# Boundary chains of four token blocks emitted one step behind each other, with last groups of four k-tiles and two-block splits

## The chip, the cores and the metric

One core of one Trainium2 chip runs the whole program. The metric is the time of one execution in device microseconds (us). Engines are named as in the profile: PE (TensorE matmul), PEld (its weight loads), DVE (VectorE), ACT (ScalarE), POOL (GpSimd), SP (SyncE, which issues most DMA). The profile lists PE's granted clock as a share of full speed: 1.00 and 0.50 are 2.4 and 1.2 GHz.

## The reference, cut to what matters

512 tokens of 1024 values go through two blocks of two layers each. That makes eight stages in a row, each ending in a projection back to 1024 values:

```
x = x + rmsnorm(ssd(rmsnorm(x)))        # ssd    first block: the stage's output is normalised
x = x + rmsnorm(conv_ffn(rmsnorm(x)))   # ffn0   before it is added
x = x + rmsnorm(rglru(rmsnorm(x)))      # lru
x = x + rmsnorm(conv_ffn(rmsnorm(x)))   # ffn1
h = h + even(rmsnorm(h))                # even   second block: plain residual
h = h + conv_ffn_2(rmsnorm(h))          # ffn2
h = h + mla(rmsnorm(h))                 # mla
h = h + conv_ffn_2(rmsnorm(h))          # ffn3
out = rmsnorm(h)
```

So between any two stages every token needs the sum of its squares over all 1024 values before the next stage's first matmul can use it. At the ends of ssd, ffn0, lru and ffn1 it needs that twice in a row: once over the stage's output, once over the new x. These four are called the double boundaries below, the ends of even, ffn2 and mla the single ones.

## The kernel before, in words

**Matmuls.** Each fp32 operand is split into a high and a low fp32r part, and a product is three passes: high by high, low by high, high by low (`mm3`, L413 to L417, weights stationary, tokens moving; `mmt`, L534 to L536, tokens stationary, used for the down projections `dn`).

**Weights.** The class `Weights` (`W`) streams chunks of 1 MB in a fixed order on SP's queue. `_half` casts half of a chunk to its high part `wh` (L283 on ACT, or L285 on DVE) and subtracts for the low part `wl` (L286 on DVE or POOL). `W.main` says on which engines, by a list of two-letter plans: the first letter is the engine of `wh`, the second that of `wl` (a is ACT, v is DVE, g is POOL). The default is `av`; lru has `vg`. The parts live in a pool of seven buffers (`wsp`), so they are made only shortly before use.

**Down projections.** A stage's projection back is summed over k-tiles of 128 rows in groups (`G_SSD`, `G_LRU`, `G_FF` and so on). All groups but the last are added into `acc` (or into `x` in the second block) over all tokens. The last group has two k-tiles at most boundaries and is done by `last_down` one block q of 128 tokens at a time, two halves of 512 columns each.

**The boundary.** `stage_end` does, for each token block q: the last group's matmuls `dn(q)`; the add into `acc` on DVE (L411); the sum of squares on ACT (`sq`, L494, one instruction for each half); the inverse root on POOL (`rr`, L496 and L497); `nx` on DVE (L592) and the add to x (L411); squares of x, `rr` again; the normalised block `n` on ACT (L513); eight 128x128 transposes on PE (L516); and the split of each transposed tile into `xh` on ACT (L521) and `xl` on DVE (L522), 128x128 each. At single boundaries the chain is shorter: `dn` is added to x, then squares, `rr`, `n`, transposes, splits. The next stage's first three weight tiles (`units`) are then multiplied in two halves of 256 tokens: half 0 needs blocks 0 and 1, half 1 needs blocks 2 and 3.

Emission order in the code before is:

```
dn(0) dn(1) newx(0) dn(2) newx(1) dn(3) newx(2)
units, half 0        newx(3)        units, half 1
```

where `newx(q)` is the whole chain of block q from its squares of `acc` to its splits. A scheduler may move instructions past one another where tiles allow it, but on each engine the four blocks' chains stand largely one after another.

**Other places.** At the start, x is loaded on SP between the first weight halves, and the same transposes, splits and units follow. At the end, `final_end` does the last projection and the output norm block by block.

Of the kernel before, what the change touches and what calls it, by code (L numbers as in the profile page):

```python
# [16 lines left out]
P = 128  # L17
# [230 lines left out]
class Weights:  # L248


    def __init__(self, c, ap):
        self.c, self.ap, self.n = c, ap, ap.shape[0]
        self.used, self.count, self.halves, self.raw = [], {}, [], None
        self.look, self.done = 2, 0
        self.main = self.plan = ("av",)
        self.until = 0

# [13 lines left out]
    def _half(self):  # L271
# [5 lines left out]
        hi = c.wsp.tile([P, T], F32R, name="wh", tag="wh")  # L277
        lo = c.wsp.tile([P, T], F32R, name="wl", tag="wl")
# [11 lines left out]
    def ahead(self, n):  # L290
        while self.done < min(n, 2 * self.n):
            self._half()

# [38 lines left out]
def build(tc, nc, aps, at, stages):  # L332
# [4 lines left out]
    with ExitStack() as st:  # L337
# [25 lines left out]
        for q in range(4):  # L363
            for h in range(2):
                nc.sync.dma_start(x[q][:, h * T:h * T + T], aps["x"][q][:, h * T:h * T + T])
            W.load_half(q)
# [123 lines left out]
        def rms_rows(src):  # L490

            ss = small.tile([P, 2], F32, name="ss", tag="ss")
            for h in range(2):
                A.activation(tmp("sq"), src[h], AF.Square, scale=1.0 / 32, accum_out=ss[:, h:h + 1])  # L494
# [5 lines left out]
        class Entry:  # L500
# [7 lines left out]
            def put(self, q):  # L508
                rr = rms_rows([half(x, q, h) for h in range(2)])
                qs = slice(q * P, q * P + P)  # L510
                for h in range(2):
                    n = tmp("n")
                    A.activation(n, half(x, q, h), AF.Identity, scale=rr)  # L513
                    ps = mmps(c.tp)
                    for e in range(4):
                        PE.transpose(ps[:, e * P:e * P + P], n[:, e * P:e * P + P], ident)  # L516
                    for e in range(4):
                        hi, lo = self.xs[4 * h + e]
                        gk = vc(self.gain, 4 * h + e)
                        pe = ps[:, e * P:e * P + P]  # L520
                        A.activation(hi[:, qs], pe, AF.Identity, scale=gk)  # L521
                        V.scalar_tensor_tensor(lo[:, qs], pe, gk, hi[:, qs].bitcast(F32),  # L522
                                               op0=ALU.mult, op1=ALU.subtract)

        def units_half(uc, up, xs, h):
            for u, ps in zip(uc, up):
                for k in range(KD):
                    mm3(ps[:, HALF[h]], u.blk(k), cut(xs[k], HALF[h]), k == 0, k == KD - 1)
# [37 lines left out]
        def last_down(name, hs, acc):  # L566

            n = len(hs)
            W.look = 0
            c.dn = "dn" if "dn" in c.psb else "ax"  # L570
            ws = parts_of(name, 2 * n)

            def dn(q):
                for h in range(2):
                    ps = mmps(c.dn)
                    for k in range(n):
                        mmt(ps, hs[k], q, ws[n * h + k], k == 0, k == n - 1)
                    tt(half(acc, q, h), ps, half(acc, q, h), ALU.add)
            return dn

        def stage_end(name, hs, acc, g, nxt, units, xo=None):
# [3 lines left out]
            dn = last_down(name, hs, acc)  # L585

            def newx(q):
                if g is not None:
                    rr = rms_rows([half(acc, q, h) for h in range(2)])
                    for h in range(2):  # L590
                        t = tmp("nx")
                        V.scalar_tensor_tensor(t, half(acc, q, h), rr, g[h],  # L592
                                               op0=ALU.mult, op1=ALU.mult)
                        tt(half(x, q, h), t, xo[2 * q + h] if xo else half(x, q, h), ALU.add)
                nxt.put(q)
# [12 lines left out]
            W.look = 2  # L608
            return up

        def final_end(name, hs):
# [4 lines left out]
            def outs(q):  # L616
                rr = rms_rows([half(x, q, h) for h in range(2)])
                for h in range(2):
                    o = tmp("o")
                    V.scalar_tensor_tensor(o, half(x, q, h), rr, g[h],  # L620
                                           op0=ALU.mult, op1=ALU.mult)
                    nc.sync.dma_start(aps["out"][q][:, h * T:h * T + T], o)
            for q in range(4):
                dn(q)
                outs(q)
# [44 lines left out]
        def ssd(pl, ent, pre, fin):  # L670
# [101 lines left out]
            def core(g, qd, bc, xc, zs, gated):  # L772
# [97 lines left out]
                if g < 3:  # L870
                    def dn():
                        for n, d in enumerate(down("sout", hs, acc, copy_first if g == 0 else None)):

# [3 lines left out]
                else:  # L877
                    drain(down("sout", hs[:2], acc))
                    st_.hs = hs[2:]
# [46 lines left out]
            for k in range(8):  # L926
                t = pl.tile([P, T], F32, name="xo", tag="zs" if k < 7 else "xc", bufs=7 if k < 7 else 5)
# [5 lines left out]
        def lru(pl, ent, pre, fin):  # L933
# [67 lines left out]
            def dense():  # L1001
# [11 lines left out]
                for q, grp in enumerate((range(4), range(4, 8), range(8, 10))):  # L1013
# [3 lines left out]
                    for h in grp:  # L1017
# [5 lines left out]
                        hs.append(split(pl, t, "hs", bufs=7))  # L1023
# [800 lines left out]
```

## Time and profile before

| what | value |
|---|---|
| time, median of 3 runs | 2987.62 us (2987.57 to 2993.34) |
| profiled execution, time | 2990.36 us |
| its span | 2988.6 us |
| mean granted PE clock | 0.979 |
| PE busy | 2870.8 us, 96% |
| DVE busy | 1878.0 us, 63% |
| ACT busy | 1291.0 us, 43% |
| POOL busy | 416.6 us, 14% |

The profiled execution is 2.74 us above the median of the runs; its own time and its span differ by 1.8 us, which lie around the program. PE is busy nearly all the time, so time can come out of the program only where PE waits, where its clock is granted at the lower level, or where it does less work.

### The profile page before, as it was taken

The page shows a single profiled execution, that of the slowest core. Times are in us where ns is not written, and L with a number is a line of the kernel's source. Part 1 is how long each engine was busy: PE and PEld are TensorE (multiplying, and loading weights), DVE is VectorE, ACT ScalarE, POOL GpSimd, SP SyncE. Part 2 cuts the span into 40 slices and gives each one's busy share as a digit, 9 for nine tenths or more (in the row PEclk, how much of TensorE's full clock was granted, in tenths as well). Part 3 has the DMA queues.
Part 4 walks back from the last instruction along what each step waited for, and adds up shares of the span by engine and source line. Part 5 has one row for each costly group of instructions (what it writes and reads, how often), then busy time and mean ns, then how long its engine had stood idle before and what let it go on. Part 6 is the DMA issues. An engine that isn't in the chain of part 4 may idle for free.

```text
span 2988.6 us, 35753 instructions
## 1 busy us (share of the span) xinstructions
PE 2870.8 (96%) x13528; PEld 2347.7 (79%) x13528; DVE 1878.0 (63%) x3120; ACT 1291.0 (43%) x2366; POOL 416.6 (14%) x524
## 2 busy tenths in 40 slices
PE   8999997999999799799999998999999999999998
PEld 7767777888888677688878877888888876788887
DVE  6887776555655786586665764666545566655544
ACT  5444445433333562444333444655333364453332
POOL 1233210000000146302342311100000000000000
PEclk8999998999999899899999998999999999999999
DMA  3212231222222122123333334622222220132222
GB/s 135 71 57 71 71 106 71 99 98 89 96 99 99 64 85 99 61 103 109 111 135 121 124 114 146 196 82 85 99 99 99 85 89 29 57 105 93 99 88 89
DMA packets 100188, 285.74 MB, mean 96 GB/s; under 512 B 19632, under 2 KB 28336, under 8 KB 99504
## 3 DMA queue, kind: packets, MB, share of 16 engines
q1 hardware_dynamic: 89376, 272.15, 26.0%
q10 hardware_dynamic: 10640, 11.30, 1.2%
q8 instruction: 107, 1.75, 0.2%
q14 instruction: 65, 0.53, 0.1%
HBM read 269.31 MB, written 14.12 MB: 95 GB/s over the span
## 4 chain that ended last, share of the span: by engine, by line
PE 86%; DVE 7%; ACT 4%; POOL 2%; issue 1%; DMA 1%; SPq 0%; DVEq 0%; POOLq 0%; ACTq 0%
PE mm L415 18%; PE mm L416 17%; PE mm L417 17%; PE dn L535 6%; PE dn L534 6%; PE dn L536 6%; PE mm L534 2%; PE mm L535 2%; PE mm L536 2%; ACT sq L494 1%; ACT n L513 1%; DVE wl L286 1%; POOL rr L497 1%; PE ax L1656 1%; PE ax L1678 1%
## 5 line engine op out<-in xcount | busy, mean ns | idle before, releaser
L283 ACT CAST wh<-raw 128x512 fp32r<-128x512 f32 x870 | 537.5, 622 | 1114.8 <-PE mm L416 711.5
L415 PE MATMUL mm<-xh,wh 128*128 128x512 f32 (+1 forms) x2600 | 982.7, 381 | 5.5 <-DVE co L633 3.4
L417 PE MATMUL mm<-xh,wl 128*128 128x512 f32 (+1 forms) x2600 | 980.5, 378 | 7.5 <-POOL wl L286 7.5
L416 PE MATMUL mm<-xl,wh 128*128 128x512 f32 (+1 forms) x2600 | 980.1, 378 | 2.7 <-DVE xl L522 2.7
L286 DVE TENSOR_TENSOR wl<-raw,wh 128x512 fp32r<-128x512 f32 x870 | 633.8, 735 | 501.2 <-ACT wh L283 485.4
L415 PEld LDWEIGHTS mm<-xh,wh 128*128 128x128 f32 x2600 | 496.3, 192 | 99.7 <-issue 7.3
L417 PEld LDWEIGHTS mm<-xh,wl 128*128 128x128 f32 x2600 | 496.9, 191 | 96.9 <-POOL wl L286 8.8
L416 PEld LDWEIGHTS mm<-xl,wh 128*128 128x128 f32 x2600 | 496.8, 191 | 90.7 <-DVE xl L522 3.8
L534 PE MATMUL dn<-wh,hsh 128*128 128x512 f32 x864 | 339.3, 393 | 2.6 <-DVE acc L411 2.6
L535 PE MATMUL dn<-wl,hsh 128*128 128x512 f32 x864 | 340.7, 394 | 0.3 <-DVE wl L286 0.3
L536 PE MATMUL dn<-wh,hsl 128*128 128x512 f32 x864 | 335.8, 389 | 0.0
L496 POOL TENSOR_SCALAR rr<-ss 128x1 f32<-128x1 f32 x52 | 16.3, 314 | 1554.8 <-ACT sq L494 1554.7
L534 PEld LDWEIGHTS dn<-wh,hsh 128*128 128x128 f32 x864 | 162.2, 188 | 41.0 <-DVE acc L411 3.0
L536 PEld LDWEIGHTS dn<-wh,hsl 128*128 128x128 f32 x864 | 162.2, 188 | 35.9
L535 PEld LDWEIGHTS dn<-wl,hsh 128*128 128x128 f32 x864 | 162.5, 188 | 32.9 <-DVE wl L286 0.7
L633 DVE SCALAR_TENSOR_TENSOR ca<-mm,vec,ca 128x510 f32<-128x510 f32 x216 | 161.6, 748 | 16.1 <-ACT ca L630 12.5
L411 DVE TENSOR_TENSOR acc<-dn,acc 128x512 f32<-128x512 f32 x128 | 87.6, 686 | 83.7 <-PE dn L536 83.4
L411 DVE TENSOR_TENSOR x<-dn,x 128x512 f32<-128x512 f32 x96 | 66.0, 689 | 101.6 <-PE dn L536 101.6
L286 POOL TENSOR_TENSOR wl<-raw,wh 128x512 fp32r<-128x512 f32 x66 | 104.2, 1597 | 92.5 <-DVE wh L285 73.0
L633 DVE SCALAR_TENSOR_TENSOR cb<-mm,vec,cb 128x510 f32<-128x510 f32 (+1 forms) x128 | 95.7, 748 | 9.8 <-ACT cb L630 7.9
L429 ACT CAST hsh<-act 128x512 fp32r<-128x512 f32 x108 | 67.2, 622 | 77.9 <-DVE act L411 77.8
L630 ACT ACTIVATE ca<-mm,vec 128x512 f32<-128x512 f32 x108 | 83.8, 776 | 11.3 <-PE mm L417 11.3
(482 smaller groups left out, 3284.9 us busy)
## 6 DMA issues: line engine op xcount, KB each, us to landing
raw<-w SPq DMA_DIRECT2D x233, 1024.0 KB, 4.8
sD<-s5t SPq DMA_DIRECT2D x4, 1024.0 KB, 7.4
row<-rows SPq DMA_DIRECT2D x12, 256.0 KB, 5.2
sR<-s5t SPq DMA_DIRECT2D x4, 768.0 KB, 4.3
x<-x SPq DMA_DIRECT2D x8, 256.0 KB, 5.5
xo<-x ACTq DMA_DIRECT2D x8, 256.0 KB, 3.4
s5t<-el ACTq DMA_DIRECT2D x8, 256.0 KB, 3.2
s5t<-HD ACTq DMA_DIRECT2D x4, 512.0 KB, 3.1
```

Source lines behind the costliest of these rows:

```text
L283: c.nc.scalar.copy(hi, r)
L286: (c.nc.gpsimd if e[1] == "g" else c.nc.vector).tensor_tensor(lo, r, hi.bitcast(F32), op=ALU.subtract)
L411: (eng or V).tensor_tensor(o, a, b, op=op)
L415: PE.matmul(ps, lhsT=wh, rhs=xh, start=first, stop=False)
L416: PE.matmul(ps, lhsT=wh, rhs=xl, start=False, stop=False)
L417: PE.matmul(ps, lhsT=wl, rhs=xh, start=False, stop=last)
L429: A.copy(hi, src)
L534: PE.matmul(ps, lhsT=hh[:, qs], rhs=wh, start=first, stop=False)
L535: PE.matmul(ps, lhsT=hh[:, qs], rhs=wl, start=False, stop=False)
L536: PE.matmul(ps, lhsT=hl[:, qs], rhs=wh, start=False, stop=last)
L630: A.activation(o, src, AF.Identity, scale=w[nt - 1], bias=b)
L633: V.scalar_tensor_tensor(o[:, d:], src[:, :T - d], w[j], o[:, d:], op0=ALU.mult, op1=ALU.add)
```

## The change

The work is the same: the same matmuls, the same norms, the same splits. What differs is where it stands:

- **Last groups.** `G_SSD` goes from (4, 4, 4, 2, 2) to (4, 4, 4, 4), `G_LRU` from (4, 4, 2) to (4, 2, 4), ffn0 and ffn1 end in a group of four k-tiles in place of two groups of two. The other lists are as they were, so at the single boundaries the last group still has two.
- **Homes for weights.** A last group of four needs eight weight halves at once, more than the pool's seven buffers. `reserve` and `last_homes` give them tiles of the stage that are free by then, and `W.more()` makes the parts ahead, one or two with each step of the group before.
- **stage_end** is taken apart into `a` (matmuls, add, squares of one half), `b` (nx, x, squares), `n`, `t` (transposes) and `parts` (splits), and these are emitted so that each block stands one step behind the block before it.
- **Transposes** of two token blocks go into the same four PSUM tiles, two k-tiles to a tile, and `parts(h)` splits 128x256 at a time: 8 on ACT and 8 on DVE for each half of the tokens, where there were 16 and 16 of 128x128.
- **units**: at double boundaries the transposes of block 2 stand between the second and third unit of half 0; at single ones after the first unit.
- **Start and end**: x is loaded two blocks ahead of each pair of weight halves, and the pieces are emitted like a boundary; in `final_end` the output of a block stands after the next block's first half.
- **lru's plan** goes from `vg` to `av` and `vv` in turn: `wl` always on DVE, `wh` half on ACT, half on DVE.

```diff
-G_SSD = _groups(4, 4, 4, 2, 2)
-G_LRU = _groups(4, 4, 2)
+G_SSD = _groups(4, 4, 4, 4)
+G_LRU = _groups(4, 2, 4)
-G_FF = {FF1: _groups(*(4,) * 7, 2, 2), FF2: _groups(*(4,) * 5, 2)}
+G_FF = {FF1: _groups(*(4,) * 8), FF2: _groups(*(4,) * 5, 2)}
...
+    def reserve(self, n, tiles):
+
+        for k, t in enumerate(tiles):
+            self.homes[2 * n + k] = t
...
-        hi = c.wsp.tile([P, T], F32R, name="wh", tag="wh")
-        lo = c.wsp.tile([P, T], F32R, name="wl", tag="wl")
+        if h in self.homes:
+            hi, lo = self.homes.pop(h)()
+        else:
+            hi = c.wsp.tile([P, T], F32R, name="wh", tag="wh")
+            lo = c.wsp.tile([P, T], F32R, name="wl", tag="wl")
...
+    def more(self, n=1):
+        self.ahead(self.done + n)
...
+            def turn(self, q, n):
+
+                if q % 2 == 0:
+                    self.tp = [mmps(t) for t in c.tp[q // 2]]
                 for k in range(KD):
+                    o = (k % 2) * 256 + (q % 2) * P
+                    PE.transpose(self.tp[k // 2][:, o:o + P], n[k // 4][:, (k % 4) * P:(k % 4) * P + P], ident)
+
+            def parts(self, h):
+                for k in range(KD):
+                    hi, lo = self.xs[k]
+                    gk = vc(self.gain, k)
+                    pe = self.tp[k // 2][:, (k % 2) * 256:(k % 2) * 256 + 256]
+                    A.activation(hi[:, HALF[h]], pe, AF.Identity, scale=gk)
+                    V.scalar_tensor_tensor(lo[:, HALF[h]], pe, gk, hi[:, HALF[h]].bitcast(F32),
+                                           op0=ALU.mult, op1=ALU.subtract)
...
-            dn(0)
-            dn(1)
-            newx(0)
-            dn(2)
-            newx(1)
-            dn(3)
-            newx(2)
-            uc = [W.next(u) for u in units]
-            up = [mmps() for _ in units]
-            units_half(uc, up, nxt.xs, 0)
-            newx(3)
-            units_half(uc, up, nxt.xs, 1)
-            W.look = 2
-            return up
...
+            if g is not None:
+                a(0, 0), a(0, 1), a(1, 0), b(0), a(1, 1), n(0), a(2, 0), b(1), a(2, 1), t(0), n(1)
+                a(3, 0), t(1), b(2), a(3, 1), nxt.parts(0), n(2), b(3)
+
+                def rest():
+                    n(3), t(3), nxt.parts(1)
+                return first_units(nxt, units, [lambda: None, lambda: t(2)], rest)
+            a(0, 0), a(0, 1), a(1, 0), n(0), a(1, 1), a(2, 0), t(0), n(1), a(2, 1), a(3, 0), t(1)
+            n(2), nxt.parts(0), a(3, 1), n(3)
+
+            def rest():
+                t(3), nxt.parts(1)
+            return first_units(nxt, units, [lambda: t(2)], rest)
...
-        PLAN = {"lru": ("vg",)}
+        PLAN = {"lru": ("av", "vv")}
```

**ACT at the boundary from ffn0 to lru.** In the kernel before, these rows stand together; x1 and acc2 are token blocks 1 and 2, `n_8144` and `n_8159` are the two halves of block 1's normalised x:

```order
L494 ACTIVATE sq_8137,ss_8136<-x1_83 128x512
L494 ACTIVATE sq_8139,ss_8136<-x1_83 128x512
L513 ACTIVATE n_8144<-x1_83,rr_8141 128x512
L513 ACTIVATE n_8159<-x1_83,rr_8141 128x512
L494 ACTIVATE sq_8191,ss_8190<-acc2_4325 128x512
L494 ACTIVATE sq_8193,ss_8190<-acc2_4325 128x512
L521 ACTIVATE xh0_4301<-ax_8146,vec_81 128x128
L521 ACTIVATE xh4_4309<-ax_8161,vec_81 128x128
```

The squares of block 2's `acc` stand behind block 1's `n`. In the changed kernel ACT has, at the same place:

```order
L531 ACTIVATE n_7972<-x0_82,rr_7946 128x512
L531 ACTIVATE n_7974<-x0_82,rr_7946 128x512
L506 ACTIVATE sq_7991,ss_7976<-acc2_4261 128x512
L506 ACTIVATE sq_8001,ss_7997<-x1_83 128x512
L506 ACTIVATE sq_8006,ss_7997<-x1_83 128x512
L506 ACTIVATE sq_8025,ss_7976<-acc2_4261 128x512
L531 ACTIVATE n_8046<-x1_83,rr_8008 128x512
L531 ACTIVATE n_8048<-x1_83,rr_8008 128x512
```

Block 2's squares now stand ahead of block 1's `n`. A little later on ACT, the splits of half 0 and block 2's `n` stand so:

```order
L548 ACTIVATE xh3_4243<-mm_8035,vec_81 128x256
L506 ACTIVATE sq_8084,ss_8075<-x2_84 128x512
L506 ACTIVATE sq_8103,ss_8050<-acc3_4262 128x512
L531 ACTIVATE n_8124<-x2_84,rr_8086 128x512
L531 ACTIVATE n_8126<-x2_84,rr_8086 128x512
L548 ACTIVATE xh5_4247<-mm_8036,vec_81 128x256
L548 ACTIVATE xh7_4251<-ax_8037,vec_81 128x256
```

Two of the eight splits that half 0 needs, xh5 and xh7, come behind block 2's `n`.

**PE at the boundary from ffn0 to lru.** Before, the last down matmuls and the transposes of blocks 0 and 1 stand directly ahead of the first unit:

```order
L536 MATMUL dn<-wh,hsl 128x512
L516 MATMUL ax<-ident,n 128x128 x4
L534 MATMUL dn<-wh,hsh 128x512
L516 MATMUL ax<-ident,n 128x128 x4
L535 MATMUL dn<-wl,hsh 128x512
L536 MATMUL dn<-wh,hsl 128x512
L516 MATMUL ax<-ident,n 128x128 x8
L415 MATMUL mm<-xh_4301,wh 128x256 x3
```

All down matmuls are used up by the time that block 1's eight transposes come. In the changed kernel the end of the down projection reads:

```order
L560 MATMUL dn<-w_7836,hsh 128x512
L561 MATMUL dn<-w_7836,hsh 128x512
L562 MATMUL dn<-w_7836,hsl 128x512
L541 MATMUL mm<-ident,n 128x128 x6
L541 MATMUL ax<-ident,n 128x128 x2
L560 MATMUL dn<-w_7853,hsh 128x512
L561 MATMUL dn<-w_7853,hsh 128x512
L562 MATMUL dn<-w_7853,hsl 128x512
L560 MATMUL dn<-w_7862,hsh 128x512
L561 MATMUL dn<-w_7862,hsh 128x512
L562 MATMUL dn<-w_7862,hsl 128x512
```

Block 1's transposes are shown here; three more down matmuls follow these rows, then the first unit. Block 0's transposes stand 15 down matmuls further ahead, with 72 down matmuls (all of blocks 0, 1 and 2) ahead of them.

**PE at the single boundary from ffn2 to mla.** Before, between block 1's transposes and the first unit:

```order
L535 MATMUL dn<-wl,hsh 128x512
L516 MATMUL ax<-ident,n 128x128 x8
L536 MATMUL dn<-wh,hsl 128x512
L534 MATMUL dn<-wh,hsh 128x512
L535 MATMUL dn<-wl,hsh 128x512
L536 MATMUL dn<-wh,hsl 128x512
L415 MATMUL mm<-xh_17112,wh 128x256 x2
L416 MATMUL mm<-xl_17113,wh 128x256
```

In the changed kernel:

```order
L541 MATMUL mm<-ident,n 128x128 x6
L541 MATMUL ax<-ident,n 128x128 x2
L560 MATMUL dn<-wh,hsh 128x512
L561 MATMUL dn<-wl,hsh 128x512
L562 MATMUL dn<-wh,hsl 128x512
L560 MATMUL dn<-wh,hsh 128x512
L561 MATMUL dn<-wl,hsh 128x512
L562 MATMUL dn<-wh,hsl 128x512
L541 MATMUL ax<-ident,n 128x128 x2
L541 MATMUL dn<-ident,n 128x128 x4
L429 MATMUL mm<-xh_16866,wh 128x256
```

Six of the transposes of block 2 have come ahead of the first unit, behind only six down matmuls.

## Rows read from the trace of the kernel before

**Rows 1.** The page's busy time of each engine, share, instructions.

```profile
PE 2870.8 (96%) x13528; PEld 2347.7 (79%) x13528; DVE 1878.0 (63%) x3120; ACT 1291.0 (43%) x2366; POOL 416.6 (14%) x524
```

**Rows 2.** Windows of boundaries: us; busy PE, PEld, DVE, ACT, POOL; clock; DMA; GB/s.

```profile
435.00:490.00 55.00, 38.83 (x225) 34.80 (x224) 34.08 (x73) 33.44 (x86) 7.40 (x16) 0.81 0.13 48
987.00:1042.00 55.00, 37.35 (x223) 33.26 (x221) 38.10 (x98) 31.19 (x81) 13.35 (x21) 0.84 0.13 43
1207.00:1269.00 62.00, 42.33 (x227) 37.65 (x227) 33.79 (x82) 34.29 (x87) 17.51 (x31) 0.78 0.15 52
1776.00:1832.00 56.00, 40.17 (x229) 36.26 (x228) 35.04 (x81) 32.40 (x85) 7.71 (x18) 0.82 0.26 90
2015.00:2051.00 36.00, 34.22 (x229) 30.11 (x228) 23.90 (x55) 27.33 (x69) 3.45 (x8) 1.00 0.18 61
2383.00:2419.00 36.00, 35.05 (x229) 30.59 (x228) 26.18 (x62) 27.42 (x71) 4.86 (x18) 1.00 0.28 92
```

**Rows 3.** PE's waits, whole run: total us, times, longest.

```profile
PE ax L516 <- ACT n L513: 51.8, 17, 8.7
PE y L516 <- ACT n L513: 19.9, 4, 9.1
PE mm L417 <- POOL wl L286: 7.5, 3, 5.3
PE y L516 <- DVE xl L522: 6.0, 2, 3.3
```

**Rows 4.** ACT's timeline, ffn0 to lru: start, duration, instruction, [idle before].

```profile
997.07 1.34 ACT L513 ACTIVATE n<-x,rr 128x512 f32<-128x512 f32 x2 [0.56 <-POOL rr L497]
...
1007.35 1.33 ACT L513 ACTIVATE n<-x,rr 128x512 f32<-128x512 f32 x2 [1.07 <-POOL rr L497]
1008.59 0.61 ACT L494 ACTIVATE sq<-acc 128x512 f32<-128x512 f32 x1
```

**Rows 5.** DVE's timeline there: the adds of block 2.

```profile
995.14 1.28 DVE L411 TENSOR_TENSOR acc<-dn,acc 128x512 f32<-128x512 f32 x2
```

**Rows 6.** PE's timeline there: block 1's transposes.

```profile
1008.12 1.97 PE L516 MATMUL ax<-ident,n 128*128 128x128 f32 x8 [8.48 <-ACT n L513]
```

**Rows 7.** Three windows in lru, one at ffn2's end; columns as in Rows 2.

```profile
1040.00:1140.00 100.00, 90.44 (x371) 72.60 (x372) 84.66 (x126) 62.82 (x87) 51.45 (x31) 0.95 0.26 90
1140.00:1210.00 70.00, 70.00 (x304) 56.87 (x304) 42.35 (x61) 8.10 (x13) 41.01 (x28) 1.00 0.30 107
1088.00:1092.00 4.00, 2.14 (x5) 1.46 (x6) 2.72 (x6) 3.82 (x6) 3.78 (x3) 0.79 0.01 4
2399.00:2403.00 4.00, 3.92 (x27) 3.27 (x27) 3.40 (x9) 4.00 (x12) 0.68 (x4) 1.00 0.78 266
```

**Rows 8.** Groups of instructions, whole run: busy us, mean ns, idle before and releasers.

```profile
L521 ACT ACTIVATE xh<-ax,vec 128x128 fp32r<-128x128 f32 x192 | 62.8, 365 | 25.1 <-DVE xl L522 17.2 <-PE ax L516 6.9
L522 DVE SCALAR_TENSOR_TENSOR xl<-ax,vec,xh 128x128 fp32r<-128x128 f32 x192 | 60.7, 345 | 36.9 <-ACT xh L521 35.7
L816 ACT COPY ent<-ax 128x256 f32<-128x256 f32 x8 | 2.9, 368 | 3.5 <-PE ax L813 3.5
L633 DVE SCALAR_TENSOR_TENSOR ca<-mm,vec,ca 128x511 f32<-128x511 f32 x108 | 80.9, 749 | 3.3
L283 ACT CAST wh<-raw 128x512 fp32r<-128x512 f32 x870 | 537.5, 622 | 1114.8 <-PE mm L416 711.5 <-PE dn L536 304.0 <-PE mm L536 34.6
L286 DVE TENSOR_TENSOR wl<-raw,wh 128x512 fp32r<-128x512 f32 x870 | 633.8, 735 | 501.2 <-ACT wh L283 485.4 <-PE ax L1208 8.8 <-PE ax L781 3.2
L286 POOL TENSOR_TENSOR wl<-raw,wh 128x512 fp32r<-128x512 f32 x66 | 104.2, 1597 | 92.5 <-DVE wh L285 73.0 <-DVE spp L649 7.6 <-PE ax L417 5.1
L411 DVE TENSOR_TENSOR gt<-gt,th 128x512 f32<-128x512 f32 x10 | 9.7, 1009 | 0.0
L993 DVE SCALAR_TENSOR_TENSOR th<-at,th 128x512 f32<-128x512 f32 x10 | 12.5, 1292 | 8.7 <-ACT th L992 8.7
L411 DVE TENSOR_TENSOR act<-act,cb 128x512 f32<-128x512 f32 x64 | 46.0, 719 | 6.2 <-DVE cb L633 0.5
```

More of the change, by code (lines that the diff above doesn't have):

```diff
@@ L488, in rstd, with squares, new_ss, rms_of @@
             return r
[L490 to L494, printed above, removed]
+        def squares(src, h, ss):
+            A.activation(tmp("sq"), src, AF.Square, scale=1.0 / 32, accum_out=ss[:, h:h + 1])
+        def new_ss():
+            return small.tile([P, 2], F32, name="ss", tag="ss")
+        def rms_of(ss):
             rr = small.tile([P, 1], F32, name="rr", tag="rr")
@@ L506, in __init__, with norm @@
                             main.tile([P, T], F32R, name=f"xl{k}", tag=f"xl{k}")) for k in range(KD)]
-            def put(self, q):
-                rr = rms_rows([half(x, q, h) for h in range(2)])
-                qs = slice(q * P, q * P + P)
+            def norm(self, q, rr):
+                out = []
                 for h in range(2):
@@ L569, in last_down, with dn, first_units @@
             W.look = 0
+            ws = parts_of(name, 2 * n)
             c.dn = "dn" if "dn" in c.psb else "ax"
[L571 to L578, printed above, removed]
-            return dn
+            def dn(q, h, ss):
+                ps = mmps(c.dn)
+                for k in range(n):
+                    mmt(ps, hs[k], q, ws[n * h + k], k == 0, k == n - 1)
+                tt(half(acc, q, h), ps, half(acc, q, h), ALU.add)
+                squares(half(acc, q, h), h, ss)
+            return dn
+        def first_units(nxt, names, between, after):
+            uc = [W.next(u) for u in names]
+            up = [mmps() for _ in names]
+            for u, ps in zip(uc, up):
+                unit_half(u, ps, nxt.xs, 0)
+                if between:
+                    between.pop(0)()
+            after()
+            for u, ps in zip(uc, up):
+                unit_half(u, ps, nxt.xs, 1)
+            W.look = 2
+            W.more(2)
+            return up
         def stage_end(name, hs, acc, g, nxt, units, xo=None):
@@ L585, in stage_end @@
             dn = last_down(name, hs, acc)
[L587 to L595, printed above, removed]
@@ new lines, in b, with n, t @@
+            def b(q):
+                s2 = new_ss()
+                for h in range(2):
+                    t = tmp("nx")
+                    V.scalar_tensor_tensor(t, half(acc, q, h), r1[q], g[h], op0=ALU.mult, op1=ALU.mult)
+                    tt(half(x, q, h), t, xo[2 * q + h] if xo else half(x, q, h), ALU.add)
+                    squares(half(x, q, h), h, s2)
+                r2[q] = rms_of(s2)
+            def n(q):
+                ns[q] = nxt.norm(q, r2[q])
+            def t(q):
+                nxt.turn(q, ns[q])
@@ L1012, in dense @@
                 prev = None
[L1013 removed]
+                for q, grp in enumerate(G_LRU):
                     hs = []
@@ L1746, in up, with last_homes, one, f @@
                 return split(pl, act, "hs", bufs=8)
+            def last_homes():
+                def one(k):
+                    def f():
+                        if n == 1 and k < 2:
+                            t = pl.tile([P, 2, T], F32R, name="w2", tag=("HD", "W_")[k], bufs=1)
+                        else:
+                            t = pl.tile([P, 2, T], F32R, name=f"w2{k}")
+                        return t[:, 0], t[:, 1]
+                    return f
+                return [one(k) for k in range(8 if n == 0 else 4)]
             prev = None
@@ L1752, in ffn @@
                     hs.append(up(b))
+                if block == 1 and q == len(G_FF[nb]) - 1:
+                    W.reserve(len(W.used) + len(prev), last_homes())
                 if prev is not None:
@@ L1756, in ffn @@
                             step()
+                        if block == 1 and q == len(G_FF[nb]) - 1:
+                            W.more()
                 prev = hs
```

100 lines of the change are left out of this document (69 added, 31 removed).

## The prediction

> **What bounds the kernel now.** I read the busy times first: PE is busy for 2870.8 us [rows 1], so only what PE waits, or does at a lower clock, can come out. The list of PE's waits says where: 51.8 and 19.9 us in front of the transposes, waiting for `n` on ACT [rows 3]. They lie at the boundaries, so I took windows of these, cut so that each holds nearly the same work (223 to 229 matmuls). The two single boundaries shown take 36 us at a clock of 1.00; the four double ones take 55, 55, 62 and 56 us at 0.78 to 0.84 [rows 2]. That is 228 us against 4 x 36 = 144: **84 us** is the most that can come out of the double boundaries. Two things make it up. PE stands idle, and even its busy time is longer for as many matmuls: 38.83, 37.35, 42.33 and 40.17 us, 39.7 in the mean, against 34.6 in the mean of the single ones, so the low clock costs about 5 us at each.
>
> Why PE stands idle shows in the chain at ffn0 to lru. Block 2's sums were added to `acc` by 996.4 [rows 5], but their squares began at 1008.59, behind block 1's `n` [rows 4]. So a block's chain starts only when the chain before it ends: from block 0's `n` to block 1's is 1007.35 - 997.07 = 10.3 us [rows 4], and PE, which has used up its down matmuls, stands 8.48 us in front of block 1's transposes [rows 6]. The bound is one chain of 10.3 us after another, not any engine's throughput: in that window DVE is busy 38.10 of 55 us, ACT 31.19 [rows 2].
>
> **The change, part by part.** *Chains overlapped, groups of four.* In the new ACT order block 2's squares are ahead of block 1's `n`, so chains can run side by side, at PE's pace. The pace: 304 matmuls of 512 columns in 70.00 us [rows 7] are 0.230 us each; a token block of the last group is now 24 of them, 5.5 us, where it was 12. I count from the first of these at ffn0 to lru, with 10.3 us for a chain, loaded as it is now, and 0.7 for the add ahead of it.
> - Block 0's down matmuls end at 5.5, its `n` at 16.5; PE gets to its transposes behind 72 matmuls, at 16.6. No wait.
> - Eight transposes took 1.97 us at the low clock [rows 6]; I take 1.0 at the full one. With 15 more down matmuls PE is at block 1's at 21.0; that `n` is due at 11.0 + 11.0 = 22.0. Wait 1.0.
> - The last nine down matmuls end at 25.1. The first unit wants a PSUM bank that the transposes used, so two k-tiles must be split first. A split of 128x256 has no row: ACT's copy of that shape took 368 ns, against 365 for the split of 128x128; DVE's lies between 345 (128x128) and 749 ns (511 columns), about 0.48 in proportion [rows 8]. With squares in between that makes some 1.9 us of wait. xh5 and xh7 stand behind block 2's `n` on ACT, due at 27.6 and later: about 1.2 us more. So stalled, PE is about 3 us late, and next to wait would be block 2's transposes; they stand behind two units, where their `n` is done.
> - 72 unit matmuls of 256 columns at half of 0.230, and block 2's transposes, take PE to about 37.5; block 3's `n` is due at 25.1 + 11.0 = 36.1, no wait. Its transposes, 0.9 us for the first split, and 8.3 us of half 1 end at 47.7.
> - 48 of the 96 down matmuls stood ahead of the window before, 11.0 us. That leaves 36.7 us.
>
> For the clock I add 3 us, since waits of 1 to 2 us remain: **40**, against 55. The bounds are 0 and 8.1 (42.33 - 34.22, the most that a window lost [rows 2]). lru to ffn1 has the same order: 40. At ssd to ffn0 and ffn1 to even, three and four weight casts still stand between the chains; four of 0.735 us on DVE [rows 8] are 2.9: 43 each. Together 166 in place of 228: **-62 us**; bounds -84 (all at 36) and -40 (rival 3).
>
> *The clock, weighed.* Of short waits the rows say both: around a wait of 1.73 us in lru the clock was 0.79, while a stretch of ffn2's end with PE busy 3.92 of 4 us kept 1.00 [rows 7]. The Trainium skill, "TensorE: Matmul & The Clock Gate", section "A second HAM failure mode: psum-queue depth-cycling", says that a PE which idles briefly between groups of matmuls, as it goes through PSUM banks, can have its clock swing between half and full. This change does just that with its transposes' banks; by the page alone the sum would be nearer rival 2 than mine.
>
> *Splits two blocks wide.* They take 32 instructions on ACT and on DVE to 16 at each boundary: 32 x 0.365 = 11.7 us of ACT become about 6 to 7, DVE 11.0 become 7.7. Both engines work beside PE, so it counts only as relief within the walk above. What it costs: a split now waits for the second block's transposes.
>
> *Single boundaries.* Their last groups are unchanged and their chains already overlap: at 36 us with 34.22 busy there is little to gain. But in the new order block 2's transposes come ahead of the first unit behind six down matmuls. A block is 12 matmuls, 2.8 us, so PE is there about 13 us from the first, while I count block 2's `n` for 15; and the splits stand behind that. Up to 3 us each, less what PE idles there now (36.00 - 34.22 = 1.8): I take **+4** for the three, bounds 0 and +9.
>
> *Start.* PE waits 6.0 us for splits to free the transposes' one bank [rows 3]; four banks for two blocks remove that, but half 0 now needs splits of both blocks: **-4**, bounds -7 and 0.
>
> *lru's plan.* POOL's `wl` takes 1597 ns, and PE waited 7.5 us in all for it [rows 3, 8]. On DVE it costs 735. In the first 100 us of lru POOL was busy 51.45, some 30 of these; DVE, busy 84.66 [rows 7], gets 30 x 0.735 = 22 us and gives 15 casts to ACT, at least 15 x 0.5 = 7.5. That is +14.5 and would fill it. But DVE runs slower beside POOL: `gt` 1009 ns against 719 for a like operation, `th` 1292 against 749 [rows 8], ten each, so 8.3 us come back, and others of the kind some 2 more. About +4 on DVE, of which 3 may reach PE: -7 + 3 = **-4**; bounds -12 (its waits, the clock after them, PE's other idling) and +14.5. ACT has 62.82 of 100, and room. From 1140 on, DVE is at 42.35 of 70: no matter.
>
> *Nothing.* The homes hide behind the group before (16 more casts and subtractions moved, none added), as does the earlier raw DMA; bare, eight subtractions of 0.735 would cost 5.9 us a boundary. The end's order saves nothing: the last block's chain still follows the last matmul.
>
> **Sum:** -62 + 4 - 4 - 4 = **-66**. The profiled execution took 2990.4 us, 2.7 above the median, so 2924 for such a one, and **2922** beside the median of 2987.6.
>
> **The rivals.** *1, everything closes:* the double boundaries come down to the 36 us of the single ones, and lru's 7.5 and the start's 6.0 us go too: -97.5, **2890**. For it: DVE and ACT are busy at most 38.10 of 55 us now [rows 2]. Against it: squeezed to 36 us, DVE's 38.10, less 3.3 by the wider splits, would nearly fill the time, and xh5 and xh7 stand behind `n`.
> *2, the clock stays down:* the new small waits cost at each double boundary the worst that one lost, 8.1 us and not 3: +20, **2942**; with 5 us at each single one as well, 2957. For it: 0.79 at a 1.73 us wait. Against: 1.00 at ffn2's end.
> *3, the chains stay serial* at 10.3 us each, because ACT's or DVE's queue holds one chain behind another: block 0's `n` ends at 16.5, block 3's at 47.4, half 1 at 58.6, less 11.0 is 47.6 for a mean of 57: -38 and not -62, **2946**. Against it: the order rows.
> *4, DVE becomes lru's bound:* +14.5 where I took -4: **2940**. It fails if `gt` and `th` come down to about 0.72.
> *5, slower:* the double boundaries run at half clock. Their work is 96 x 0.230 + 144 x 0.115 + 4 = 43 us at full clock; each us of it done at half takes one more. From 66 / 4 = 16.5 us, 38% of it, the gain is gone; at 60% it is 4 x 25.8 - 66 = +37, **3025**. Only a clock that falls under a steady row of matmuls does that, and no row shows one.
>
> **Chances.** My forecast 0.52 (its own range 2903 to 2937), rival 1 0.13, 2 0.14, 3 0.08, 4 0.06, 5 0.04, something unseen 0.03. A change within 0.2%, 6 us, is what a measurement here can't tell from none. All cases but the fifth and part of the last are faster: 0.93; within: 0.02; slower: 0.05. The range is from 2895, which leaves out half of rival 1, to 2955, which leaves out rival 5 and the worst of 2.
>
> **What would show it.** Right: windows of the double boundaries, cut alike, at 40 to 43 us; waits for `n` from 71.7 us to under 15; no wait for POOL's `wl`; clock over 0.9 there; `gt` near 0.72 us. Wrong: a clock of 0.8 in these windows with few waits (rival 2), 10 us from `n` to `n` (rival 3), DVE above 95 of 100 in lru (rival 4), new waits for `xh` of more than 3 us a boundary.

## The result: 2924.2 us, and the profile after

| | before | changed |
|---|---|---|
| time, median | 2987.86 us (4 runs) | 2924.2 us (4 runs, 2921.57 to 2925.5) |
| ratio | | 0.9782, 95% interval 0.9765 to 0.9799 |
| profiled execution | 2990.36 us, span 2988.6 | 2921.57 us, span 2919.8 |
| mean granted PE clock | 0.979 | 0.991 |

The kernel became 64 us faster where 66 was forecast. The total hides two errors that cancel: the double boundaries gave some 15 us more than forecast, and lru lost 9 us where a gain of 4 was forecast.

The page's busy times of the changed kernel, to be held against [rows 1]:

```profile
PE 2849.1 (98%) x13528; PEld 2328.5 (80%) x13528; DVE 1845.0 (63%) x3001; ACT 1285.7 (44%) x2273; POOL 314.3 (11%) x458
```

PE has as many matmuls as before and is busy 21.7 us less; they are the same matmuls, run less often at the low clock. The other 47 us of the span came out of waiting.

Windows of the seven boundaries in the changed kernel, columns as in [rows 2], whose six rows the first six answer to:

```profile
430.50:466.60 36.10, 33.50 (x226) 29.89 (x225) 24.93 (x45) 25.62 (x61) 6.02 (x14) 1.00 0.11 38
963.00:1000.00 37.00, 33.61 (x226) 29.77 (x224) 27.41 (x69) 24.54 (x58) 6.05 (x14) 1.00 0.02 5
1175.60:1212.60 37.00, 33.98 (x229) 30.31 (x228) 25.61 (x54) 26.61 (x62) 7.99 (x23) 1.00 0.09 31
1721.00:1760.50 39.50, 34.88 (x227) 31.47 (x227) 27.14 (x57) 26.03 (x62) 6.62 (x16) 0.96 0.35 120
1946.00:1981.00 35.00, 33.33 (x224) 29.60 (x223) 20.34 (x38) 23.35 (x52) 3.45 (x8) 1.00 0.17 61
2314.00:2350.40 36.40, 34.62 (x224) 31.08 (x224) 25.51 (x48) 25.00 (x57) 5.25 (x18) 0.95 0.27 95
2531.00:2565.40 34.40, 32.76 (x221) 29.13 (x220) 19.82 (x37) 23.14 (x51) 3.44 (x8) 1.00 0.18 62
```

The four double boundaries, 55 to 62 us before at a clock of 0.78 to 0.84, now take 36 to 39.5 us, three of them at 1.00: about what a single boundary takes. Counted alike in both traces, from the first start to the last end of the 224 matmuls that close with half 1 of the first units, they took 55.3, 53.5, 61.8 and 55.5 us before and take 36.2, 36.8, 36.4 and 39.3: **-77 us**. The single ones went from 106.1 to 107.8 us for the three: +2, nearly all of it at ffn2 to mla (35.4 to 36.8, its clock at 0.95). The end of the first units of the program came at 43.5 us before and at 38.6 now: -5. From the end of the units of ffn0 to lru to the next such count, lru took 166.8 us before and takes 176.2: **+9**. That makes -71; the remaining +2 of the -68.8 us between the two spans lies mostly in ffn1 (+1.5) and ssd (+0.7).

PE's longest waits in the changed kernel, whole run, columns as in [rows 3]:

```profile
PE mm L429 <- DVE xl L549: 11.8, 8, 4.2
PE mm L431 <- DVE wl L295: 10.8, 3, 3.6
PE mm L541 <- ACT n L531: 7.1, 5, 3.9
PE mm L429 <- ACT wh L292: 6.1, 2, 3.4
PE y L888 <- DVE sc L425: 4.7, 5, 1.8
PE ax L541 <- ACT n L531: 3.2, 3, 1.1
```

Waits of transposes for `n`, 71.7 us before, are 10.3 us here (7.1 + 3.2), of which 5.6 stand at the start of the program and 1.5 at the double boundaries. In their place the first units of the double boundaries wait for `xl`, 1.5 to 4.2 us each. POOL's `wl` is gone from the list, and two new rows have come, both in lru: `wl` from DVE and `wh` from ACT, 16.9 us together where POOL's `wl` had cost 7.5.

That the chains overlap shows on ACT. At ffn0 to lru the four blocks' `n` now follow one another by 6.3 to 6.5 us, where [rows 4] had 10.3:

```profile
966.41 1.34 ACT L531 ACTIVATE n<-x,rr 128x512 f32<-128x512 f32 x2 [0.46 <-POOL rr L515]
...
972.75 1.33 ACT L531 ACTIVATE n<-x,rr 128x512 f32<-128x512 f32 x2 [0.46 <-POOL rr L515]
...
979.17 1.34 ACT L531 ACTIVATE n<-x,rr 128x512 f32<-128x512 f32 x2 [0.46 <-POOL rr L515]
...
985.62 1.34 ACT L531 ACTIVATE n<-x,rr 128x512 f32<-128x512 f32 x2 [1.10 <-POOL rr L515]
```

At the same boundary, PE's waits in time order, to be held against the 8.48 us of [rows 6]:

```profile
973.53 1.05 PE L541 MATMUL mm<-ident,n 128*128 128x128 f32 x6 [0.51 <-ACT n L531]
...
978.36 0.39 PE L429 MATMUL mm<-xh,wh 128*128 128x256 f32 x1 [1.48 <-DVE xl L549]
980.92 0.39 PE L429 MATMUL mm<-xh,wh 128*128 128x256 f32 x1 [0.38 <-ACT xh L548]
...
991.02 0.39 PE L430 MATMUL mm<-xl,wh 128*128 128x256 f32 x1 [0.86 <-DVE xl L549]
```

These are the four waits of the forecast, in its order: for block 1's `n` (forecast 1.0), for two split k-tiles to free the unit's bank (1.9), for `xh5` behind block 2's `n` (1.2), for the first split of half 1 (0.9). The clock does not fall: it is 1.00 over the whole window (963 to 1000 above).

In lru, first ACT's timeline around 1030:

```profile
1027.82 0.61 ACT L443 CAST xbh<-co 128x512 fp32r<-128x512 f32 x1
1028.45 1.28 ACT L1066 ACT_TABLE_LOAD   x1
1029.74 1.15 ACT L1066 ACTIVATE th<-th 128x512 f32<-128x512 f32 x2
1030.80 0.60 ACT L292 CAST wh<-raw 128x512 fp32r<-128x512 f32 x1
```

PE's timeline at the same place:

```profile
1031.45 0.50 PE L429 MATMUL mm<-xh,wh 128*128 128x512 f32 x1 [3.38 <-ACT wh L292]
1031.79 0.39 PE L430 MATMUL mm<-xl,wh 128*128 128x512 f32 x1
1035.79 0.80 PE L431 MATMUL mm<-xh,wl 128*128 128x512 f32 x1 [3.60 <-DVE wl L295]
```

And DVE's, which makes the `wl` that PE waits for last:

```profile
1030.40 1.29 DVE L1067 SCALAR_TENSOR_TENSOR th<-at,th 128x512 f32<-128x512 f32 x2 [1.25 <-ACT th L1066]
1031.62 1.28 DVE L425 TENSOR_TENSOR gt<-gt,th 128x512 f32<-128x512 f32 x2
1032.82 2.33 DVE L1070 TENSOR_TENSOR_SCAN h<-at,gt 128x512 f32<-128x512 f32 x2
1035.07 0.66 DVE L295 TENSOR_TENSOR wl<-raw,wh 128x512 fp32r<-128x512 f32 x1
```

A cast of 0.60 us that PE needs at 1028 stands on ACT behind the gates' table load and activations, for which DVE waits as well. When the cast is done, its `wl` has missed its turn on DVE and stands behind `th`, `gt` and two scans, 4.9 us in all. PE waits for each in turn, 7 us in all, then does a few matmuls at the low clock (0.80 us and 0.63 after it). The same pair of waits comes again at 1093 and 1098, and one for `wl` alone, 3.60 us, at 1058.

### The profile page after: what moved, and what is told of

It is laid out like the page before. It is cut to its first block, busy times and chain, and to the rows that moved or that the text cites. A ratio compares the mean times of both kernels' runs of the same rounds, so it can differ in the third digit from the quotient of the medians.

```text
span 2919.8 us, 35383 instructions
## 1 busy us (share of the span) xinstructions
PE 2849.1 (98%) x13528; PEld 2328.5 (80%) x13528; DVE 1845.0 (63%) x3001; ACT 1285.7 (44%) x2273; POOL 314.3 (11%) x458
## 4 chain that ended last, share of the span: by engine, by line
PE 76%; DVE 4%; ACT 3%; issue 1%; POOL 1%; DMA 0%; DVEq 0%; POOLq 0%; ACTq 0%
PE mm L429 16%; PE mm L430 16%; PE mm L431 16%; PE dn L561 6%; PE dn L560 6%; PE dn L562 6%; PE mm L562 1%; PE mm L560 1%; PE mm L561 1%; PE ax L1744 1%; PE ax L1766 1%; ACT sq L506 1%; DVE wl L295 1%; PE ax L1743 1%; DVE x L425 1%
## 5 line engine op out<-in xcount | busy, mean ns | idle before, releaser
L292 ACT CAST wh<-raw 128x512 fp32r<-128x512 f32 x889 | 548.9, 622 | 1135.3 <-PE mm L430 719.0
L295 DVE TENSOR_TENSOR wl<-raw,wh 128x512 fp32r<-128x512 f32 x922 | 667.7, 731 | 511.1 <-ACT wh L292 495.0
L560 PE MATMUL dn<-wh,hsh 128*128 128x512 f32 x816 | 321.1, 394 | 2.6 <-DVE acc L425 2.6
L561 PE MATMUL dn<-wl,hsh 128*128 128x512 f32 x816 | 322.2, 395 | 0.2 <-DVE wl L295 0.2
L562 PE MATMUL dn<-wh,hsl 128*128 128x512 f32 x816 | 317.5, 389 | 0.0
L560 PEld LDWEIGHTS dn<-wh,hsh 128*128 128x128 f32 x816 | 153.4, 188 | 38.9 <-DVE acc L425 3.0
L562 PEld LDWEIGHTS dn<-wh,hsl 128*128 128x128 f32 x816 | 153.6, 188 | 34.3
L561 PEld LDWEIGHTS dn<-wl,hsh 128*128 128x128 f32 x816 | 153.8, 189 | 31.2 <-DVE wl L295 0.7
L425 DVE TENSOR_TENSOR acc<-dn,acc 128x512 f32<-128x512 f32 x112 | 76.9, 687 | 88.5 <-PE dn L562 88.1
L425 DVE TENSOR_TENSOR hsl<-act,hsh 128x512 fp32r<-128x512 f32 x108 | 79.8, 739 | 10.6 <-ACT hsh L443 2.7
```

The lines of the kernel that those rows point to most:

```text
L292: c.nc.scalar.copy(hi, r)
L295: (c.nc.gpsimd if e[1] == "g" else c.nc.vector).tensor_tensor(lo, r, hi.bitcast(F32), op=ALU.subtract)
L425: (eng or V).tensor_tensor(o, a, b, op=op)
L560: PE.matmul(ps, lhsT=hh[:, qs], rhs=wh, start=first, stop=False)
L561: PE.matmul(ps, lhsT=hh[:, qs], rhs=wl, start=False, stop=False)
L562: PE.matmul(ps, lhsT=hl[:, qs], rhs=wh, start=False, stop=last)
```

## The experiments

All times are medians; the kernel before took 2989.81 us beside the first four and 2988.39 beside the last four.

**lru's plan put back.** The changed kernel with

```diff
-        PLAN = {"lru": ("av", "vv")}
+        PLAN = {"lru": ("vg",)}
```

> The changed kernel with lru's plan put back to vg (wh on DVE, wl on POOL); all else as changed. From the end of the units of the boundary ffn0 to lru to the boundary lru to ffn1, the changed kernel took 176.0 us, the kernel before 167.3. Theory A: the plan did it, because wh on ACT stands behind the gates' function-table load and activations, and wl on DVE behind the gates' scans: then this stretch returns to about 167, the waits of 3.4, 3.6, 2.7 and 3.6 us for wh (ACT) and wl (DVE) go, the waits for POOL's wl come back, and the time is some 8 us less than the changed kernel's, about 2916. Theory B: the new group order 4, 2, 4 and the splits made ahead into homes did it: the stretch stays near 176, the time within 3 us of 2924. Theory C, the prediction's term: the plan gains 4 us, so the time is 2928.

2921.11 us, ratio 0.9773 (0.9759 to 0.9788); that can't be told from the changed kernel's 0.9782. By the trace, lru took 173.5 us: 2.7 less than with the new plan, 6.7 more than in the kernel before with the same plan. PE's waits in lru were

```profile
PE mm L431 <- POOL wl L295: 7.0, 2, 5.3
PE mm L560 <- ACT t L1094: 4.1, 1, 4.1
PE mm L429 <- DVE co L693: 2.8, 3, 1.7
```

None of the three theories holds alone. POOL's waits come back as A says, but this plan together with the changed kernel's lru has a wait of its own: a down matmul waits 4.1 us for ACT's `t` (L1094, the gelu of a k-tile of the group). Neither the kernel before with this plan nor the changed kernel with its own has it. Whether the group order 4, 2, 4 or the weight parts made ahead bring it was not tested.

**lru's parts all on DVE.** The changed kernel with `PLAN = {"lru": ("vv",)}`.

> The changed kernel with lru's plan vv (wh and wl both on DVE). If it is ACT's queue that is late (wh behind the table load), the waits for wh (6.1 us in two) go, and with them part of the waits for wl that follow on them: 5 to 8 us less than the changed kernel, about 2917. If it is DVE's queue that is late (wl behind th, gt and the scans), DVE only gets 15 more casts of 0.42 us, and the time is the same or up to 6 us more, 2924 to 2930.

2905.4 us, ratio 0.9716 (0.9702 to 0.9731), 19 us less than the changed kernel and more than expected. lru took 157.3 us. Its first 100 us:

```profile
1003.00:1103.00 100.00, 95.94 (x412) 78.11 (x411) 95.99 (x172) 65.80 (x91) 0.00 (x0) 0.98 0.29 100
```

Against the changed kernel's

```profile
1000.00:1100.00 100.00, 82.63 (x331) 65.38 (x332) 79.42 (x135) 69.75 (x102) 0.00 (x0) 0.90 0.22 78
```

So ACT's queue was what came late. With no cast on it PE does 412 matmuls where it did 331, at 0.98 instead of 0.90, and DVE, with more to do, is busy for 95.99 us without holding PE up. The waits for `wh` are gone, and of three for `wl` one of 3.5 us is left.

**Groups of two.** The changed kernel with the groups of before and no homes:

```diff
-G_SSD = _groups(4, 4, 4, 4)
-G_LRU = _groups(4, 2, 4)
+G_SSD = _groups(4, 4, 4, 2, 2)
+G_LRU = _groups(4, 4, 2)
...
-                    st_.hs = hs
+                    drain(down("sout", hs[:2], acc))
+                    st_.hs = hs[2:]
```

(ffn0's and ffn1's groups likewise; calls of `reserve` and of `more` in the group before are out.)

> The changed kernel with the groups of the kernel before (last groups of two k-tiles), without homes and without splits ahead in the group before; chains, transposes, splits and plan as changed. Theory A, the chain needs the cover of 5.5 us of matmuls to a block: with 2.76 us to a block, block 0's n is due at 13.8 us where PE comes at 8.3, and one or two more waits follow: 6 to 8 us at each of the four double boundaries, so 2948 to 2956, with waits for n on PE of over 25 us. Rival: overlapping the chains alone does it, and the deeper groups add nothing: within 5 us of 2924.

2961.32 us, ratio 0.9905 (0.9888 to 0.9921). The double boundaries, counted as above, took 47.3, 46.6, 47.8 and 47.0 us, waits for `n` 34.9 us over ten. At ssd to ffn0:

```profile
441.79 1.54 PE L541 MATMUL mm<-ident,n 128*128 128x128 f32 x6 [2.36 <-ACT n L531]
448.67 1.54 PE L541 MATMUL mm<-ident,n 128*128 128x128 f32 x6 [4.92 <-ACT n L531]
452.91 0.58 PE L429 MATMUL mm<-xh,wh 128*128 128x256 f32 x1 [2.27 <-DVE xl L549]
```

Theory A: the chains need the cover of 24 matmuls a block. It cost 10 us a boundary and not 6 to 8. PE's waits grew by 6.5 us a boundary (39.1 against 13.2 us over the four), as expected; the rest is the clock: six transposes take 1.54 us here, 0.82 in the changed kernel's block 0, and these windows ran at 0.82 to 0.86.

At ffn0 to lru the first two steps from `n` to `n` are 6.9 and 6.4 us here, about as in the changed kernel:

```profile
984.46 1.33 ACT L531 ACTIVATE n<-x,rr 128x512 f32<-128x512 f32 x2 [0.80 <-POOL rr L515]
...
991.34 1.33 ACT L531 ACTIVATE n<-x,rr 128x512 f32<-128x512 f32 x2 [0.46 <-POOL rr L515]
...
997.77 0.72 ACT L531 ACTIVATE n<-x,rr 128x512 f32<-128x512 f32 x1 [0.47 <-POOL rr L515]
```

So overlapped chains still need some 6.5 us a block when PE brings half the work. Of the prediction's own figures, 24 matmuls (5.5 us) and eight transposes (1.0) just fill that, 12 do not. What holds the step at 6.5 us was not tested.

**Serial chains.** The changed kernel with the double boundaries emitted one chain after another:

```diff
+            if g is not None:
+                both(0), both(1), newx(0), both(2), newx(1), nxt.parts(0), both(3), newx(2)
+
+                def rest():
+                    newx(3), nxt.parts(1)
+                return first_units(nxt, units, [], rest)
```

(`both` does a block's matmuls and adds, `newx` its squares, `b`, `n` and `t`. So block 2's transposes also stand ahead of the first unit again.)

> The changed kernel with the four double boundaries' chains emitted one after another, as before (a block's squares of acc behind the n of the block before it), with groups of four, homes and two-block splits kept. Theory A, the serial chain of 10.3 us a block was the bound: block 3's n comes at about 47 us from the first down matmul, half 1 ends at 58, 10 us later than in the changed kernel, at each of four boundaries: 2960 to 2975, and a clock below 0.9 in these windows. Rival: the cover of four k-tiles is what matters and the order is not: within 10 us of 2924.

2953.32 us, ratio 0.988 (0.9865 to 0.9895). The double boundaries took 45.3, 43.6, 42.1 and 45.9 us, 28 more than in the changed kernel, at clocks of 0.88 to 0.93. From `n` to `n` a block takes 8.4 to 13.4 us. The order matters as theory A says, but less than the 36 us or more expected: the longest wait is one of 4 to 7 us for block 3's `n`, at three of the four places above 5, while blocks 0 to 2 are mostly covered by the four k-tiles. So of 77 us at the double boundaries, undoing the groups alone gives 40 back and undoing the order alone 28; neither part does it by itself.

**lru's new plan in the kernel before.** One line:

```diff
-        PLAN = {"lru": ("vg",)}
+        PLAN = {"lru": ("av", "vv")}
```

> The kernel before with lru's plan av and vv in turn, nothing else. This is the term of the prediction alone: -4 us, about 2984, by it. Theory A, from the run with groups of two, where lru with this plan took 177.9 us from the units of one boundary to the next against 166.8 before: +9 to +11, about 2998, with waits for wh on ACT of about 6 us and for wl on DVE of about 10 in lru, in place of 7.5 for POOL's wl. Rival: the loss comes only together with the overlapped boundary: within 3 us of before.

2995.73 us, ratio 1.0024 (1.0014 to 1.0033): 7.3 us slower. lru took 176.9 us in place of 166.8 (the boundary behind it took 3.7 less), and the waits were those of the changed kernel, one for one:

```profile
PE mm L417 <- DVE wl L286: 10.9, 3, 3.7
...
PE mm L415 <- ACT wh L283: 6.1, 2, 3.4
```

Theory A. The loss needs nothing of the new boundary.

**All on DVE in the kernel before.** `PLAN = {"lru": ("vv",)}` there.

> The kernel before with lru's plan vv, nothing else. If lru loses time only because weight parts stand behind the gates' table loads on ACT or beside slow POOL, the stretch of 166.8 us falls to about 157 as it did in the changed kernel with this plan: 2977 to 2980, and DVE is busy over 90 of the first 100 us. If DVE is the bound in lru of the kernel before (rival 4 of the prediction, its DVE gets 22 us more), the stretch grows by 5 us or more: over 2993.

2980.48 us, ratio 0.9972 (0.9962 to 0.9983): 7.9 us faster. lru took 157.6 us, as in the changed kernel with this plan, with DVE busy for 96.75 of its first 100 us:

```profile
1040.00:1140.00 100.00, 96.34 (x414) 78.75 (x415) 96.75 (x175) 66.75 (x93) 0.00 (x0) 0.98 0.28 102
```

With this plan the stretch does not depend on the group order. A full DVE is no bound here, since what PE needs from it comes early enough.

**Splits of 128x128.** The changed kernel with each split made as two:

```diff
-                    A.activation(hi[:, HALF[h]], pe, AF.Identity, scale=gk)
-                    V.scalar_tensor_tensor(lo[:, HALF[h]], pe, gk, hi[:, HALF[h]].bitcast(F32),
-                                           op0=ALU.mult, op1=ALU.subtract)
+                    for e in range(2):
+                        pe = self.tp[k // 2][:, (k % 2) * 256 + e * P:(k % 2) * 256 + e * P + P]
+                        qs = slice(h * 256 + e * P, h * 256 + e * P + P)
+                        A.activation(hi[:, qs], pe, AF.Identity, scale=gk)
+                        V.scalar_tensor_tensor(lo[:, qs], pe, gk, hi[:, qs].bitcast(F32),
+                                               op0=ALU.mult, op1=ALU.subtract)
```

> The changed kernel with each split of 128x256 made as two of 128x128, in the same places. A split of 128x256 took 0.47 us on ACT and 0.48 on DVE, one of 128x128 0.365 and 0.345. Theory A, the splits of half 0 are on the path at the double boundaries (PE waits 1.5 to 4.2 us for xl there): the wait for the first unit grows by some 0.5 to 1 us for two k-tiles and the waits for xh by another, 1 to 2 us at each of eight places, 2932 to 2940. Rival, the width is only relief beside PE: within 4 us of 2924.

2958.39 us, ratio 0.9896 (0.9883 to 0.991): 34 us more than the changed kernel, over twice what theory A expected. It is much the same at all eight places: 3.9 to 4.8 us at the double boundaries, 3.2 to 5.4 at the single ones (40.2, 39.9 and 40.9 us), 3.6 at the start; 34 in all, the clock's share with it. (At ffn1 to even block 2's transposes came ahead of the first unit in this run, and PE waited 5.9 us for their `n` in place of `xl`.) One of those places, even to ffn2:

```profile
1981.30 1.27 PE L541 MATMUL ax<-ident,n 128*128 128x128 f32 x8 [1.19 <-ACT n L531]
1985.22 0.39 PE L429 MATMUL mm<-xh,wh 128*128 128x256 f32 x1 [2.65 <-DVE xl L551]
...
1985.77 0.41 PE L429 MATMUL mm<-xh,wh 128*128 128x256 f32 x1
```

and its clock behind that:

```profile
1985.00:1989.00 4.00, 3.78 (x19) 3.78 (x20) 2.25 (x7) 2.90 (x8) 0.56 (x1) 0.57 0.00 0
```

The changed kernel waited 1.07 and 0.31 us at this place and kept 1.00. Here the wait for `xl` is 2.65 us, the clock is 0.57 for the next 4 us, and half 1 then waits 0.83 and 0.45 us more for `xh`. The width is no relief beside PE, as long as splits of two blocks begin only when the second block's transposes are done. Splits of 128x128 that begin behind each block's own transposes, as in the kernel before, were not tried in the changed one.

**The parts that paid, together.** The changed kernel with lru's plan `vv` and two more edits, read apart by their windows:

```diff
-                if q < 3:
+                if q < 3 and 2 * q + h < ahead:
                     W.more()
...
+            ahead = 3 if name in ("sout", "down1") else 6
...
-            return first_units(nxt, units, [lambda: t(2)], rest)
+            return first_units(nxt, units, [lambda: None, lambda: t(2)], rest)
```

> The changed kernel with three edits that can be read apart by their windows: lru's plan vv; at the single boundaries block 2's transposes behind the second unit; at ssd to ffn0 and ffn1 to even only three weight halves made between the chains, the rest behind block 2's n. lru's plan alone gave 2905. Theory: block 2's transposes in front of the first unit cost the waits of 1.0 to 1.1 us for n at the single boundaries, which go; the casts cost 2.7 us of the 4.17 us wait at ffn1 to even, which falls to about 1.5: 2898 to 2902. Rival: the later weight parts are then late themselves, with new waits for wh or wl in units 1 and 2, and block 2's transposes wait for their PSUM bank instead: 2905 or more.

2902.61 us, ratio 0.9707 (0.9694 to 0.9721): the fastest of all, 21.6 us below the changed kernel. Against lru's plan alone (2905.4) it is 2.8 us, inside the two intervals. By the windows, ffn1 to even fell from 39.3 to 36.2 us, with the wait of 4.17 us for `xl` down to 1.50 and the clock back at 1.00:

```profile
1720.88 0.39 PE L429 MATMUL mm<-xh,wh 128*128 128x256 f32 x1 [1.50 <-DVE xl L549]
```

The casts that stood between the splits cost about what the prediction took for them: 2.7 us of the wait against 2.9. Little of that reaches the total, since in this trace ssd itself took 2.6 us more than with lru's plan alone (396.1 against 393.6); why is open. The edit for the single boundaries did nothing: the scheduler put block 2's transposes ahead of the first unit all the same, and they wait 1.06 us there as before. So whether that wait could go stays open.

## Why the prediction was right, and which steps were off

- **The chain, not an engine, was the bound: right.** Emitted in series, the chains give back 28 of 77 us, with too little cover 40. But overlapped chains do not run "at PE's pace" whatever it is: at ffn0 to lru their step of 6.3 to 6.9 us stays when PE has half the matmuls to do.
- **The walk at ffn0 to lru: right.** It gave 36.7 us without clock loss, and 36.8 were measured; the four waits came in the forecast order. That the number fits so well is in part luck: the waits were 3.2 us in all against 5.0, and PE took 1.8 us more than counted outside of them. The split of 128x256 was taken at 0.48 us on DVE, where it took 0.477, and at ACT's 0.37 for a copy, where it took 0.47 to 0.48.
- **"For the clock I add 3 us": mis-sized.** In the changed kernel's trace it was 0 at three of four double boundaries (1.00 after waits of up to 2.43 us). Only ffn1 to even, with a wait of 4.17 us, fell to 0.96. Part of that is chance: with lru's other two plans, which leave ssd to ffn0 as it is, the same wait of 2.43 us there went with a clock of 0.95 and 37.7 to 37.8 us. The sum forecast was 166 us for the four; the windows cut like those of [rows 2] give 149.6. Some 10 or 11 of these 16 us are the clock and 3 the casts at ssd to ffn0, which cost next to nothing (36.2 there, 36.8 at ffn0 to lru, which has no such casts). Rival 2, the swinging clock, did not come. Where waits grew it did: 0.92 to 0.96 with 128x128 splits, 0.82 to 0.86 with groups of two. The Trainium skill, "TensorE: Matmul & The Clock Gate", section "A second HAM failure mode: psum-queue depth-cycling", describes a clock that swings when PE idles briefly and often between groups of matmuls; the traces show it in these two runs, and in the changed kernel at one double boundary of four. Rival 1 described the boundaries better than my forecast, and what was held against it, a nearly full DVE, was wrong: DVE was busy for 27.41 of 37 us at ffn0 to lru. Rival 3's 58.6 lies 1 us above what the steps of the forecast's own walk give from 47.4 on, and the bound of -40 named after it should be its -38; neither carries the forecast.
- **"-7 + 3 = -4" for lru's plan: wrong.** In the kernel before it alone cost lru 10 us. In the changed kernel, where lru lost 9, going back to the old plan returns only 2.7, because a wait of 4.1 us comes with that combination. The step that failed is "ACT has 62.82 of 100, and room": a share of busy time said nothing of where the casts stand in ACT's queue. The slowdown of DVE beside POOL did go, by more than taken: `th` 1292 to 688 ns, `gt` 1009 to 683, ten each, 9.3 us; with the old plan in the changed kernel they are back at 1298 and 1010. It didn't help, since PE waited for ACT first. (The 0.5 us for a cast on DVE had no row; the 33 casts there take 0.42 in the changed kernel.) Rival 4 foresaw a loss of this order, with the wrong cause: DVE was busy for 79.42 of the 100 us, less than before. With DVE at 96 in the two runs with `vv`, lru was at its fastest.
- **Splits two blocks wide "counts only as relief": wrong in kind**, though the walk that gave the number had the width in it. With half the width in the same places 34 of the 64 us go.
- **Single boundaries and start: right in size.** +4 was forecast and +2 measured, -4 and -5. At the single ones block 2's transposes do wait, 1.04 to 1.08 us each, but two of the three boundaries lost only 0.2 us; the third, ffn2 to mla, lost 1.4 with its clock at 0.95.

## What to carry to other kernels

Free time of an engine does not show that there is room for work that another engine waits for: look at what stands ahead of it in that engine's queue at the moment when it is wanted, above all table loads, long activations and scans. A serial chain over blocks comes off the path when the blocks' chains overlap and each block brings enough matmuls to cover its step; here one without the other, both with the splits two blocks wide, gave half (37 of 77 us, overlap alone) to two thirds (49, cover alone). When work is deferred so that it can be done for two blocks at once, its width decides how late the consumer starts, and a wait that grows from one microsecond to three may also take the clock down.

## What the runs showed of the hardware beyond the forecast

After a wait of the same length, with the same matmuls directly ahead of it, the clock behaved differently from kernel to kernel. In the changed kernel a wait of 2.43 us at ssd to ffn0 was followed by a matmul of 0.39 us and then one each 0.12 us, which is full speed, and the window ran at 1.00:

```profile
446.17 0.39 PE L429 MATMUL mm<-xh,wh 128*128 128x256 f32 x1 [2.43 <-DVE xl L549]
446.39 0.28 PE L430 MATMUL mm<-xl,wh 128*128 128x256 f32 x1
446.51 0.28 PE L431 MATMUL mm<-xh,wl 128*128 128x256 f32 x1
```

With lru's parts all on DVE, which changes nothing at this boundary, the wait was 2.43 us again. Matmuls ran at full speed behind it too, but 2.4 us later at half, one each 0.21 us:

```profile
447.99 0.39 PE L429 MATMUL mm<-xh,wh 128*128 128x256 f32 x1 [2.43 <-DVE xl L549]
448.21 0.28 PE L430 MATMUL mm<-xl,wh 128*128 128x256 f32 x1
...
450.36 0.42 PE L430 MATMUL mm<-xl,wh 128*128 128x256 f32 x1
450.58 0.41 PE L431 MATMUL mm<-xh,wl 128*128 128x256 f32 x1
```

The window ran at 0.95 and took 37.7 us, 1.5 more; with lru's old plan it did the same. At ffn2 to mla it is the changed kernel that ran at 0.95, and groups of two at 1.00, with waits of 1.77 us in all in both. So a boundary gained or lost 0.8 to 1.5 us with the clock where nothing in it was changed, and no single length of wait divides full speed from half in these runs. What settles it was not found.

A function-table load held ACT for 1.28 us each time (L1066, above). The Trainium skill, "ScalarE: Activation LUTs", section "What ACT_TABLE_LOAD costs", gives about 1.283 us for the load, and the trace agrees. It adds a drain of about 1.38 us, for a total of about 2.66; at 1028.45 the trace shows none, with the cast ahead ending 0.02 us before the load and the activation behind it starting 0.01 us after. The cost to PE was larger than the load itself: it waited 3.38 us for a weight cast that stood behind one load and the two activations after it.
